# A one-column product for the sum of squares in a hybrid state-space and attention layer

## The chip, the cores and the metric

The kernel runs on one core of a Trainium2 chip. The metric is the device time of one execution in microseconds (us). Engines are named as in the profile: PE is the tensor engine, PEld its weight loads, DVE the vector engine, ACT the scalar engine, POOL GpSimd, SP the engine that issues most DMA transfers.

## The reference

One decoder layer over 2048 tokens and 16 meta tokens, 1024 features, float32. One input projection feeds two branches: a state-space scan with 16 heads in 4 groups, and gated linear attention with 4 heads. Each branch is normalised, projected, weighted with a gate and added; a last projection, the residual and a norm follow. The part around the change is the end of the state-space branch:

```python
y = jnp.concatenate([y_m, y_r], axis=1) + d_skip[:, None] * xs
y = y.reshape(b, l, D_SSD) * jax.nn.silu(z)
y_ssd = rmsnorm(y.reshape(b, l, SSD_GROUPS, D_SSD // SSD_GROUPS),
                ssd_norm_w.reshape(SSD_GROUPS, -1)).reshape(b, l, D_SSD)
```

So for each token and group the squares of 256 features are summed, and the features are scaled with the reciprocal root of their mean.

## The kernel before

The tokens are worked on in four blocks of 512. In a first half, each block goes through four state-space groups (`ssd_proj`, with `ssd_scan` for what follows a group's projections) and four attention heads (`gla_proj`, `gla_scan`). A second half, from about 1586 us on, does gates, branch projections and the output. Float32 products of the projections are made of three passes with operands split into a high and a low part (`accum`, lines 187 to 191).

The order of the first half is written with Python generators. `ssd_proj` and `gla_proj` yield after each piece, which is one projection tile of 24 passes on 512 columns in most cases. After each piece `step()` advances every scan that is under way to its next `yield`. So a `yield` in `ssd_scan` puts what follows one piece of PE's work later. PE and SP execute in the order written; for the other engines a planner that simulates the time line arranges the instructions, and each then executes in the order it was given.

A state-space group has six pieces: four projection tiles with a convolution (the last starts the scan), and two gate tiles `zs`. Its scan fetches decay rows from DRAM (`cb`, `yf`), makes the products of `bf` and `cf` for four chunks (L551), then works on the chunks one at a time (`before`, `after`: L565 to L599), and ends with the norm: features times gates (L615), squares (L616), their sum over the two tiles (L617), the sum over 128 partitions by eight passes on PE (L621, four products of float32 in two passes each, a column of ones as the moving operand), the reciprocal root (`rstd_of`, L232 on DVE and L233 on POOL), a store to DRAM and a load back that spreads the row over all partitions (L623, L625), and the last scaling (L630). Beside the scans run the gates of the attention (`gates`), the load of the next block (`load_u`) and sums for the second half (`make_sums`, whose POOL subtractions are L81).

Tiles come from pools with a fixed number of buffers: `tok4` 6, `sq` 5, `gg` 4, and three PSUM banks for each of `pj` and `pt`, two for `pc`.

Of the kernel before, what the change touches and what calls it, by code (L numbers as in the profile page):

```python
# [7 lines left out]
F32 = mybir.dt.float32  # L8
F32R = mybir.dt.float32r
# [5 lines left out]
P = 128  # L15
# [10 lines left out]
NSQ = 5  # L26
NT4 = 6
NACT = 4
NC1 = 6
LEVELS = (1, 2, 4, 8, 16, 32, 64)  # L30
NMSK = len(LEVELS)
# [10 lines left out]
def trunk_kernel(ctx: ExitStack, tc: tile.TileContext, xm, xmt, w_feat, w_tok, w_vm, w_br, w_o,  # L42
# [7 lines left out]
    def mk(pool, shape, dt, tag, **kw):  # L50
        cnt[0] += 1
        return pool.tile(shape, dt, tag=tag, name=f"{tag}_{cnt[0]}", **kw)
# [75 lines left out]
    def bank(pool, tag):  # L128
        return mk(pool, [P, 512], F32, tag)
# [100 lines left out]
    def rstd_of(ssq, n, scale):  # L230
        r = mk(sm, [P, 4], F32, "rstd")
        nc.vector.tensor_scalar(r[:, :n], ssq, scale, EPS, op0=ALU.mult, op1=ALU.add)  # L232
        nc.gpsimd.tensor_tensor(r[:, :n], r[:, :n], mhalf[:, :n], op=ALU.pow)  # L233
        return r
# [119 lines left out]
    def new_block(b, u):  # L354
        o = Block()
        o.b, o.u = b, u
        o.m0 = META if b == 0 else 0
        o.tt = o.m0 + BLK
        o.segs_all = [(0, o.tt // 2), (o.tt // 2, o.tt // 2)] if b == 0 else [(0, BLK)]
        o.segs_real = [(o.m0, BLK)]  # L360
        o.starts = [o.m0 + c * P for c in range(NCH)]
        o.chunks = ([(0, META)] if o.m0 else []) + [(a, P) for a in o.starts]
        o.ci0 = 1 if o.m0 else 0
        o.nck = len(o.chunks)
        for nm in ("tkd", "tkc", "wde", "dec"):
            setattr(o, nm, mk(bpool, [P, 5, NH], F32, nm, bufs=2))
        o.cumd = mk(dpool, [NH, BLK], F32, "cumd")
        o.ecud = mk(dpool, [NH, BLK], F32, "ecud")
        o.rstd = [mk(dpool, [P, NCH], F32, f"rstd{g}") for g in range(SG)]
        o.g_all = mk(bpool, [P, GH, META + BLK], F32, "g_all")  # L370
        o.gla = {}
        o.alr = mk(bpool, [P, 5, 48], F32, "alr")
        o.mov = lambda kt, a, n: tuple(t[:, kt, a:a + n] for t in u)
        return o


    def dt_chain(o, psd):
        m0, nck, ci0 = o.m0, o.nck, o.ci0
        tkd, tkc, wde, dec = o.tkd, o.tkc, o.wde, o.dec

        def t80(tag):
            return mk(sm, [P, 5, NH], F32, tag, bufs=1)[:, :nck]

        x = t80("dx")
        for i in range(nck):
            nc.vector.tensor_tensor(x[:, i], psd[i][:, 256:272], hv[:, 0], op=ALU.add)
            nc.scalar.activation(
                o.alr[:, i].rearrange("p (r c) -> p r c", c=16),
                psd[i][:, 272:288].unsqueeze(1).to_broadcast([P, 3, 16]), AF.Copy)
        e = t80("de")  # L390
        nc.scalar.activation(e, x, AF.Abs)
        nc.scalar.activation(e, e, AF.Exp, scale=-1.0)
        w1 = t80("dw")
        nc.vector.tensor_scalar(w1, e, 1.0, None, op0=ALU.add)
        ln = t80("dl")
        nc.scalar.activation(ln, w1, AF.Ln)
        nc.vector.scalar_tensor_tensor(e, w1, 1.0, e, op0=ALU.subtract, op1=ALU.subtract)
        nc.vector.tensor_tensor(ln, ln, e, op=ALU.subtract)
        dt = tkd[:, :nck]
        nc.vector.scalar_tensor_tensor(dt, x, 0.0, ln, op0=ALU.max, op1=ALU.add)  # L400
        nc.vector.tensor_tensor(x, dt, nega.unsqueeze(1).to_broadcast([P, nck, NH]), op=ALU.mult)
        yield
        ps = bank(pt, "pt")
        nc.tensor.matmul(ps[:, :nck * NH], tri, x.rearrange("p c h -> p (c h)"), start=True, stop=True)
        nc.vector.tensor_copy(tkc[:, :nck].rearrange("p c h -> p (c h)"), ps[:, :nck * NH])
        ps = bank(pt, "pt")
        if m0:
            nc.tensor.matmul(ps[:, :NH], ones[:META], x[:META, 0], start=True, stop=True)
        nc.tensor.matmul(ps[:, ci0 * NH:nck * NH], ones, x[:, ci0:].rearrange("p c h -> p (c h)"),
                         start=True, stop=True)  # L410
        psv = ps[:, :nck * NH].rearrange("p (c h) -> p c h", h=NH)
        nc.scalar.activation(dec[:, :nck], psv, AF.Exp)
        nc.vector.tensor_tensor(wde[:, :nck], psv, tkc[:, :nck], op=ALU.subtract)
        nc.vector.tensor_scalar(wde[:, :nck], wde[:, :nck], 0.0, None, op0=ALU.min)
        nc.scalar.activation(wde[:, :nck], wde[:, :nck], AF.Exp)
        nc.vector.tensor_tensor(wde[:, :nck], wde[:, :nck], dt, op=ALU.mult)
        yield
        ps = bank(pt, "pt")
        for c in range(NCH):
            nc.tensor.transpose(ps[:NH, c * P:(c + 1) * P], tkc[:, ci0 + c], ident)  # L420
        cr = mk(wk, [P, 3 + META + BLK], F32, "cin")[:NH, :BLK]
        nc.scalar.activation(cr, ps[:NH], AF.Copy)
        nc.scalar.dma_start(o.cumd, cr)
        er = mk(wk, [P, 3 + META + BLK], F32, "cin")[:NH, :BLK]
        nc.scalar.activation(er, ps[:NH], AF.Exp)
        nc.scalar.dma_start(o.ecud, er)
# [48 lines left out]
    def ssd_proj(o, g):  # L475
        m0, tt = o.m0, o.tt
        feats, zs = [], []
        if g == 0:
            yield from first_values(o)
        for j in range(4):  # L480
            ti = g * 4 + j
            pss = proj_feat(f"s{ti}", w_feat[T_SSD + ti], o.segs_all, o.mov)
            cin = mk(wk, [P, 3 + META + BLK], F32, "cin")
            acc = mk(wk, [P, META + BLK], F32, "acc")[:, :tt]
            nc.scalar.activation(cin[:, 0:3], tails[:, ti, :], AF.Copy)
            for ps, (a, n) in zip(pss, o.segs_all):
                nc.scalar.activation(cin[:, 3 + a:3 + a + n], ps[:, :n], AF.Copy)
                nc.scalar.activation(acc[:, a:a + n], ps[:, :n], AF.Identity, scale=hcw[:, ti, 3:4],  # L488
                                     bias=hcb[:, ti:ti + 1])
            nc.gpsimd.tensor_copy(tails[:, ti, :], cin[:, tt:tt + 3])  # L490
            for k in range(3):
                nc.vector.scalar_tensor_tensor(acc, cin[:, k:k + tt], hcw[:, ti, k:k + 1], acc,  # L492
                                               op0=ALU.mult, op1=ALU.add)
            if j % 2 == 0:
                two = pair_tile()
            f = two[:, j % 2]
            nc.scalar.activation(f[:, :tt], acc, AF.Tanh)
            nc.vector.scalar_tensor_tensor(f[:, :tt], f[:, :tt], 1.0, acc, op0=ALU.add, op1=ALU.mult)
            feats.append(f)
            if j == 3:  # L500
                begin(ssd_scan(o, g, feats, zs))
            yield
        for j in range(2):
            ti = 2 * g + j
            ps, = proj_feat(f"z{ti}", w_feat[T_Z + ti], o.segs_real, o.mov)
            zt = mk(wk, [P, BLK], F32, "gg", bufs=4)
            nc.scalar.activation(zt, ps, AF.Tanh, scale=0.5)
            nc.vector.scalar_tensor_tensor(zt, zt, 1.0, ps, op0=ALU.add, op1=ALU.mult)
            zs.append(zt)
            yield  # L510
# [7 lines left out]
    def ssd_scan(o, g, feats, zs):  # L518
# [4 lines left out]
        yf = mk(wk, [P, NCH, 256], F32, "tok4", bufs=NT4).rearrange("p c f -> p (c f)").rearrange("p (j t) -> p j t", j=2)  # L523
        for i in range(2):
            nc.scalar.dma_start(yf[64 * i:64 * i + 64], o.ecud[4 * g + i:4 * g + i + 3:2, :].unsqueeze(0).to_broadcast([64, 2, BLK]))
        yield
        hs = slice(4 * g, 4 * g + 4)

# [87 lines left out]
            nc.scalar.activation(zs[j], yf[:, j], AF.Square)  # L616
        nc.vector.tensor_tensor(zs[0], zs[0], zs[1], op=ALU.add)  # L617
        yield
        ps = bank(pt, "pt")
        for c in range(NCH):  # L620
            nc.tensor.matmul(ps[:, c:c + 1], zs[0][:, c::NCH], ones[:, :1], start=True, stop=True)  # L621
        r = rstd_of(ps[:, :NCH], NCH, 1.0 / 1024)
        nc.scalar.dma_start(o.rstd[g], r)  # L623
        rb = mk(wk, [P, BLK], F32, "gg", bufs=4)
        nc.scalar.dma_start(rb, o.rstd[g].rearrange("p c -> (p c)").unsqueeze(0).to_broadcast([P, BLK]))  # L625
        yield
        yield
# [37 lines left out]
    def gla_out_gates(o, h):  # L665
        t0 = T_GLA + 4 * h
        for j in range(2):
            ps, = proj_feat(f"g{t0 + 2 + j}", w_feat[t0 + 2 + j], o.segs_real, o.mov)
            gg = mk(wk, [P, BLK], F32, "gg", bufs=4)
            nc.scalar.activation(gg, ps, AF.Tanh, scale=0.5)  # L670
            nc.vector.scalar_tensor_tensor(gg, gg, 1.0, ps, op0=ALU.add, op1=ALU.mult)
            o.gla[h][1].append(gg)
            yield
# [566 lines left out]
```

## Time and profile before

| | us |
|---|---|
| median of 3 runs | 2375.83 (2368.9 to 2376.44) |
| the profiled execution | 2377.53 |
| its span, first to last instruction | 2375.7 |

| engine | busy us | share of the span |
|---|---|---|
| PE | 2270.2 | 96% |
| DVE | 1445.9 | 61% |
| ACT | 1091.8 | 46% |
| POOL | 679.7 | 29% |

The mean granted clock of TensorE is 0.979 of full speed. Passes on PE overlap, so that the sum of their durations is more than the busy time, and a busy PE can still be one at half clock; what a pass costs is read from the starts of one and the next. In rows of groups the numbers behind the bar are busy us, the mean ns of one instruction, and the engine's idle time before them with what ended it. In rows of waits they are us in total, times, and the longest.

### The profile page before, as it was taken

To read this page: it belongs to the slowest core of one execution; us is meant where nothing else is said; L and a number is where in the kernel's file an instruction comes from. 1 tells how busy PE (TensorE), PEld (TensorE's weight loads), DVE (VectorE), ACT (ScalarE), POOL (GpSimd) and SP (SyncE) were. 2 spreads that over 40 slices of the span, in tenths; PEclk is the share of its full clock that TensorE was granted. 3 is DMA by queue.
4 is the path that set the end of the run, shared out by engine and by line. 5 is a ranking of instruction groups with operands and counts; after the bars stand their busy time and mean duration, and the time that the engine had idled before them with its cause. 6 is when DMAs were issued, how large, how long until landed. Compare 5 with 4: busy or idle time off the path is not lost.

```text
span 2375.7 us, 34516 instructions
## 1 busy us (share of the span) xinstructions
PE 2270.2 (96%) x12009; PEld 1925.5 (81%) x12009; DVE 1445.9 (61%) x2467; ACT 1091.8 (46%) x2390; POOL 679.7 (29%) x681
## 2 busy tenths in 40 slices
PE   7999999999999999999999999979999999999998
PEld 6888888877888887888887789867888888888776
DVE  5676664466654456555356554455578854778776
ACT  4655554454433354433345333354545454554443
POOL 4343432212211112221112200027433355424231
PEclk9999999999999999999999999989999999999999
DMA  8776875777776677786587754457667876687743
GB/s 294 250 233 226 268 244 187 224 220 238 243 257 184 206 238 226 222 269 214 179 246 214 226 165 155 142 166 246 208 243 262 285 243 213 237 278 262 249 147 125
DMA packets 310877, 530.66 MB, mean 223 GB/s; under 512 B 30832, under 2 KB 146800, under 8 KB 310704
## 3 DMA queue, kind: packets, MB, share of 16 engines
q1 hardware_dynamic: 200400, 402.84, 52.6%
q10 hardware_dynamic: 110304, 125.63, 16.5%
q8 instruction: 94, 1.54, 0.3%
q14 instruction: 79, 0.65, 0.1%
HBM read 381.00 MB, written 147.36 MB: 222 GB/s over the span
## 4 chain that ended last, share of the span: by engine, by line
PE 71%; DMA 11%; DVE 6%; issue 4%; ACT 4%; POOL 2%; SPq 1%; ACTq 1%; POOLq 0%; DVEq 0%
PE pj L189 16%; PE pj L191 16%; PE pj L190 16%; PE pt L189 3%; PE pt L191 3%; PE pt L190 3%; PE pt L734 2%; DVE acc L492 2%; PE pc L190 2%; PE pc L189 2%; PE pc L191 2%; POOL wr L81 2%; DMA gg<-rstd 2%; DMA wr<-y 1%; PE pc L590 1%
## 5 line engine op out<-in xcount | busy, mean ns | idle before, releaser
L189 PE MATMUL pj<-u,whl 128*128 128x512 f32 (+1 forms) x1440 | 554.5, 385 | 6.1 <-ACT acc L488 3.9
L191 PE MATMUL pj<-u,whl 128*128 128x512 f32 (+1 forms) x1440 | 533.4, 370 | 0.8 <-POOL whl L170 0.8
L190 PE MATMUL pj<-u,whl 128*128 128x512 f32 (+1 forms) x1440 | 533.1, 370 | 0.0
L189 PEld LDWEIGHTS pj<-u,whl 128*128 128x128 f32 x1440 | 275.9, 192 | 52.5 <-ACT acc L488 5.6
L191 PEld LDWEIGHTS pj<-u,whl 128*128 128x128 f32 x1440 | 274.3, 190 | 47.7 <-POOL whl L170 1.1
L190 PEld LDWEIGHTS pj<-u,whl 128*128 128x128 f32 x1440 | 275.7, 191 | 42.4
L189 PE MATMUL pj<-b,a 128*128 128x512 f32 x640 | 254.5, 398 | 10.1 <-ACT sn L952 8.0
L190 PE MATMUL pj<-b,a 128*128 128x512 f32 x640 | 252.1, 394 | 1.8 <-DVE b L911 1.8
L191 PE MATMUL pj<-b,a 128*128 128x512 f32 x640 | 252.6, 395 | 0.0
L170 POOL TENSOR_TENSOR whl<-wr,whl 128x512 fp32r<-128x512 f32 (+1 forms) x100 | 133.4, 1339 | 191.1 <-ACT whl L169 168.5
L911 DVE TENSOR_TENSOR b<-br,b 128x512 fp32r<-128x512 f32 x196 | 152.7, 799 | 47.7 <-ACT b L910 45.2
L492 DVE SCALAR_TENSOR_TENSOR acc<-cin,hcw,acc 128x512 f32<-128x512 f32 (+1 forms) x192 | 159.9, 833 | 34.3 <-ACT acc L488 33.1
L926 POOL TENSOR_TENSOR as<-ar,ar 128x512 f32<-128x512 f32 x40 | 60.5, 1512 | 409.1 <-DMA ar<-in_w_br 151.0
L910 ACT ACTIVATE b<-br 128x512 fp32r<-128x512 f32 x196 | 119.2, 626 | 103.6 <-DMA br<-br_t 32.3
L936 DVE TENSOR_TENSOR a<-ar,a 128x512 fp32r<-128x512 f32 x160 | 126.8, 800 | 65.6 <-ACT a L935 63.5
L81 POOL TENSOR_TENSOR wr<-wr 128x256 f32<-128x256 f32 x80 | 69.0, 862 | 338.1 <-DMA wr<-y 142.6
L189 PEld LDWEIGHTS pj<-b,a 128*128 128x128 f32 x640 | 121.5, 190 | 38.5 <-ACT sn L952 10.2
L189 PE MATMUL pj<-whl,u 128*128 128x256 f32 (+1 forms) x480 | 143.7, 299 | 2.9 <-ACT u L307 1.5
L190 PEld LDWEIGHTS pj<-b,a 128*128 128x128 f32 x640 | 121.6, 190 | 29.0 <-DVE b L911 2.2
L191 PEld LDWEIGHTS pj<-b,a 128*128 128x128 f32 x640 | 121.5, 190 | 27.7
L191 PE MATMUL pj<-whl,u 128*128 128x256 f32 (+1 forms) x480 | 140.0, 292 | 1.4 <-DVE u L309 1.4
L190 PE MATMUL pj<-whl,u 128*128 128x256 f32 (+1 forms) x480 | 139.7, 291 | 0.0
(270 smaller groups left out, 4738.2 us busy)
## 6 DMA issues: line engine op xcount, KB each, us to landing
whl<-k_s SPq DMA_DIRECT2D x96, 512.0 KB, 4.5
whl<-k_g SPq DMA_DIRECT2D x96, 512.0 KB, 4.3
whl<-k_z SPq DMA_DIRECT2D x48, 512.0 KB, 3.7
wr<-in_w_feat SPq DMA_DIRECT2D x80, 256.0 KB, 4.2
whl<-k_v SPq DMA_DIRECT2D x36, 512.0 KB, 3.8
k_s<-whl SPq DMA_DIRECT2D x32, 512.0 KB, 3.5
cb<-cumd ACTq DMA_DIRECT2D x64, 256.0 KB, 5.4
k_g<-whl SPq DMA_DIRECT2D x32, 512.0 KB, 3.8
```

Source lines behind the costliest of these rows:

```text
L81: nc.gpsimd.tensor_tensor(o, x, y, op=ALU.subtract)
L170: nc.gpsimd.tensor_tensor(hl[:, 1], raw, hl[:, 0].bitcast(F32), op=ALU.subtract)
L189: nc.tensor.matmul(ps, sh, mh, start=first, stop=False, **kw)
L190: nc.tensor.matmul(ps, sh, ml, start=False, stop=False, **kw)
L191: nc.tensor.matmul(ps, sl, mh, start=False, stop=last, **kw)
L492: nc.vector.scalar_tensor_tensor(acc, cin[:, k:k + tt], hcw[:, ti, k:k + 1], acc, op0=ALU.mult, op1=ALU.add)
L590: nc.tensor.matmul(py[:, (2 + j) * P:(3 + j) * P], s_ssd[:, g, j * P:(j + 1) * P], cf[:, a:a + P], start=True, stop=True)
L734: nc.tensor.matmul(ps[:, r * P:(r + 1) * P], packed[0][:, r * P:(r + 1) * P], odd_even(half, m0 + (r + 2) * P, P // (2 * half), k_to_q - 2 ...
L910: nc.scalar.activation(t[:, 0], raw, AF.Copy)
L911: nc.vector.tensor_tensor(t[:, 1], raw, t[:, 0].bitcast(F32), op=ALU.subtract)
L926: nc.gpsimd.tensor_tensor(s1, a21, a22, op=ALU.add)
L936: nc.vector.tensor_tensor(t[:, 1], src, t[:, 0].bitcast(F32), op=ALU.subtract)
```

## The change

The sum of squares over the partitions becomes a product with one column of ones as the stationary operand, which gives a row of 512 sums. Its operand is split into a high part (ACT) and a low part (POOL) in a step of its own, and the product takes two passes. The row is copied from PSUM, stored to DRAM and loaded back as a column for each partition; `rstd_of` runs a step later on that. A `yield` more stands ahead of the scan's first products. The gate buffers become five, the decay tiles of a block have one buffer each, and three temporaries of the step-size chain use these tiles.

```diff
+NGG = 5
...
         for nm in ("tkd", "tkc", "wde", "dec"):
-            setattr(o, nm, mk(bpool, [P, 5, NH], F32, nm, bufs=2))
+            setattr(o, nm, mk(bpool, [P, 5, NH], F32, nm))
...
+        o.ssq = [mk(dpool, [P, NCH], F32, f"ssq{g}") for g in range(SG)]
...
-        e = t80("de")
+        e = wde[:, :nck]
...
-        w1 = t80("dw")
+        w1 = tkc[:, :nck]
...
-        ln = t80("dl")
+        ln = dec[:, :nck]
...
-            zt = mk(wk, [P, BLK], F32, "gg", bufs=4)
+            zt = mk(wk, [P, BLK], F32, "gg", bufs=NGG)
...
             nc.scalar.dma_start(yf[64 * i:64 * i + 64], o.ecud[4 * g + i:4 * g + i + 3:2, :].unsqueeze(0).to_broadcast([64, 2, BLK]))
+        yield
         yield
...
         nc.vector.tensor_tensor(zs[0], zs[0], zs[1], op=ALU.add)
         yield
+        sqh, sql = [mk(wk, [P, BLK], F32R, "sq", bufs=NSQ) for _ in range(2)]
+        nc.scalar.activation(sqh, zs[0], AF.Copy)
+        nc.gpsimd.tensor_tensor(sql, zs[0], sqh.bitcast(F32), op=ALU.subtract)
+        yield
         ps = bank(pt, "pt")
-        for c in range(NCH):
-            nc.tensor.matmul(ps[:, c:c + 1], zs[0][:, c::NCH], ones[:, :1], start=True, stop=True)
-        r = rstd_of(ps[:, :NCH], NCH, 1.0 / 1024)
+        for i, t in enumerate((sqh, sql)):
+            nc.tensor.matmul(ps[:1], ones_r[:, :1], t, start=i == 0, stop=i == 1)
+        rb = mk(wk, [P, BLK], F32, "gg", bufs=NGG)
+        nc.scalar.activation(rb[:1], ps[:1], AF.Copy)
+        nc.scalar.dma_start(o.ssq[g].rearrange("p c -> (p c)").unsqueeze(0), rb[:1])
+        s4 = mk(sm, [P, NCH], F32, "ssq")
+        nc.scalar.dma_start(s4, o.ssq[g])
+        yield
+        r = rstd_of(s4, NCH, 1.0 / 1024)
         nc.scalar.dma_start(o.rstd[g], r)
-        rb = mk(wk, [P, BLK], F32, "gg", bufs=4)
         nc.scalar.dma_start(rb, o.rstd[g].rearrange("p c -> (p c)").unsqueeze(0).to_broadcast([P, BLK]))
         yield
         yield
...
-            gg = mk(wk, [P, BLK], F32, "gg", bufs=4)
+            gg = mk(wk, [P, BLK], F32, "gg", bufs=NGG)
```

## The prediction

> **What bounds the kernel now.** I read the page first, then the chain, then the groups of TensorE's instructions, then the timeline around the line that the change removes, and last the clock in stretches.
>
> ```profile
> span 2375.7 us, 34516 instructions
> PE 2270.2 (96%) x12009; PEld 1925.5 (81%) x12009; DVE 1445.9 (61%) x2467; ACT 1091.8 (46%) x2390; POOL 679.7 (29%) x681
> PE 71%; DMA 11%; DVE 6%; issue 4%; ACT 4%; POOL 2%; SPq 1%; ACTq 1%; POOLq 0%; DVEq 0%
> 430.00:650.00 220.00, 213.19 (x1115) 176.01 (x1114) 132.42 (x258) 105.57 (x248) 52.27 (x76) 0.98 0.77 236
> ```
>
> The last row is the state-space stage of block 1 by itself (length, busy time of PE, its weight loads, DVE, ACT, POOL, then clock, DMA share, GB/s). PE is busy for 213 of 220 us while DVE has 132 and ACT 106. So in the stage that the change touches TensorE sets the pace, the others have room, and a microsecond taken from PE's stream there is worth about a microsecond, unless a wait of another engine reaches PE. These are the rows of PE that the change touches (busy, mean ns, then idle time before them and what ended it):
>
> ```profile
> L621 PE MATMUL pt<-ones_r,gg 128*128 128x1 f32 x128 | 30.3, 358 | 10.7 <-DVE gg L617 10.7
> L551 PE MATMUL pc<-act 128*128 128x128 f32 x128 | 22.3, 329 | 11.0 <-DVE act L498 11.0
> L779 PE MATMUL pt<-sq,ones_r 128*128 128x512 f32 x32 | 11.8, 453 | 0.0
> L587 PE MATMUL pc<-sq,c 128*64 128x128 f32 x512 | 42.1, 285 | 1.0 <-DVE sq L578 1.0
> ```
>
> The sum of squares is 128 passes with one moving column each, eight in each of 16 units (four groups in four blocks). It costs PE 30.3 us and another 10.7 us of waiting for the vector engine's sum.
>
> **Part one, the product itself.** A unit's eight passes become two passes of 512 columns against one column of ones, 32 in all. How dense such passes run is seen beside the old ones:
>
> ```profile
> 233.04 0.39 PE L189 MATMUL pj<-u,whl 128*128 128x512 f32 x1
> 233.27 0.40 PE L190 MATMUL pj<-u,whl 128*128 128x512 f32 x1
> 135.31 0.40 PE L191 MATMUL pj<-u,whl 128*128 128x512 f32 x1
> 135.54 1.80 PE L621 MATMUL pt<-ones_r,gg 128*128 128x1 f32 x8
> 137.27 0.69 PE L544 MATMUL pc<-c,bt 16*128 16x256 f32 x2
> ```
>
> A pass of 512 columns starts 0.23 us after the last; the old eight take from 135.54 to 137.27, 1.73 us. New passes at 0.23 would be 32 x 0.23 = 7.4 us; L779, which is the same form with 128 columns of ones in place of one, is 11.8 us for the same 32. No row has a single stationary column. If that were as slow again as L779 it would cost 23.6, which still is a gain. I take L779, its nearest row: 30.3 - 11.8 = 18.5 us saved, between 6.7 and 22.9.
>
> **Part two, the wait for the sum.** The three pieces put the high part (ScalarE) and the low part (GpSimd) one step of the order after the squares and the product another step later. The sum is late today in these units most of all:
>
> ```profile
> 521.48 2.03 PE L621 MATMUL pt<-ones_r,gg 128*128 128x1 f32 x8 [2.42 <-DVE gg L617]
> 901.16 2.03 PE L621 MATMUL pt<-ones_r,gg 128*128 128x1 f32 x8 [2.52 <-DVE gg L617]
> 1281.15 2.03 PE L621 MATMUL pt<-ones_r,gg 128*128 128x1 f32 x8 [3.49 <-DVE gg L617]
> L237 ACT ACTIVATE sq<-sq x16: 613/620/636, 284.1 to 1522.9; 128x512 fp32r<-128x512 f32 x16
> L170 POOL TENSOR_TENSOR whl<-wr,whl 128x512 fp32r<-128x512 f32 x92 | 126.6, 1380 | 179.4 <-ACT whl L169 156.7 <-PE pt L757 6.5 <-PE pt L191 6.1
> POOL wr L81 <- DMA wr<-y: 143.0, 19, 22.0
> ACT act L497 <- POOL wr L81: 23.1, 3, 7.7
> ```
>
> One more piece is 24 passes x 0.23 = 5.5 us of PE's time. Against it stand a copy of 0.62 and a subtraction of 1.38 us, so even the worst sum, 3.49 late, comes 5.5 - 3.49 - 2.0 = 0 us before it is needed: the 10.7 us go. The cover is thin. What is queued ahead on GpSimd is the preparation of later sums at L81, which waits for its loads, and its last row says that this has already held ScalarE for up to 7.7 us through GpSimd's queue. Price: nothing if GpSimd is free, 8 x 3 = 24 us if the low part is held by 3 us in half of the units. I take 2.
>
> **Part three, the first products a step later.** It moves L551, the transposes, the masks and everything that `before(0)` issues, the next load of `cb` on ScalarE's queue among it; the first loads stay where they are and gain 5.5 us of cover.
>
> ```profile
> PE pc L551 <- DVE act L498: 11.0, 7, 2.5
> ```
>
> PE's 11.0 us at L551 end with the vector op L498, which is at most 2.5 us late in its seven times: a whole piece covers it, and all 11.0 go. What is late next there is the vector op on these products, which nobody on PE needs for another piece.
>
> **Part four, the clock.** The stretches at half clock, in the view by stretches (length, PE busy, clock):
>
> ```profile
> 138.10:141.50 3.40, 3.40 (x17) 0.50 0.11 30
> 902.70:909.50 6.80, 6.80 (x23) 0.50 0.45 91
> 1332.80:1336.20 3.40, 3.40 (x14) 0.50 0.04 5
> sum 30.60, PE 30.11; mean PE 4.30
> 76.60:80.00 3.40, 3.40 (x12) 2.82 (x11) 2.32 (x5) 3.10 (x10) 0.30 (x1) 0.51 1.10 302
> 127.80:131.20 3.40, 3.40 (x13) 2.92 (x12) 2.70 (x6) 3.40 (x13) 0.25 (x1) 0.51 0.87 283
> ```
>
> The sum row is of seven stretches that begin during an L621 or within 1 us of its end; the last two follow a wait at L551. At half clock a stretch of dense work loses half: 30.6 / 2 = 15.3 and 6.8 / 2 = 3.4 us. I count 10 and 3, since other lulls may draw some; between 0 and 18.7. The first stretch follows passes without a wait (135.31 to 137.27 above has no idle time), so the one-column passes seem to count as little work.
>
> The Trainium skill's "TensorE: Matmul & The Clock Gate" (Part 1: The HAM clock gate) says that the clock halves after an idle window of about 3.4 us and comes back after a busy one. The stretch lengths agree; that 138.1 was drawn with no idle time does not. Read strictly, with busy instructions as busy, the rule would leave the halved stretches in place and make the sum 13 us less of a gain.
>
> **Part five, the longer way to the norm.** Instead of reading the sum from PSUM, ScalarE copies a row, stores it, loads it back as a column, and only then does the vector engine's L232 run; the store and the broadcast load of before follow. What these two DMAs cost is best told by the two that are there, the store (first row, issue to landing) and the broadcast load:
>
> ```profile
> DMA to landing us min/median/max: 1.4/2.8/5.6
> DMA to landing us min/median/max: 3.9/5.6/7.0
> DVE tok L630 <- DMA gg<-rstd: 58.5, 16, 6.1
> 673.16 1.42 DVE L630 SCALAR_TENSOR_TENSOR tok<-tok,hsw,gg 128x512 f32<-128x512 f32 x2 [4.86 <-DMA gg<-rstd]
> 676.61 0.71 PE L734 MATMUL pt<-act,c 128*128 128x128 f32 x4 [1.84 <-ACT c L728]
> 678.59 1.22 PE L734 MATMUL pt<-act,c 128*128 128x128 f32 x4 [1.27 <-ACT c L728]
> 677.40:684.20 6.80, 5.61 (x26) 5.61 (x27) 3.74 (x6) 2.30 (x5) 0.00 (x0) 0.50 0.65 251
> ```
>
> Store and load back take 2.8 + 5.6 = 8.4 us against one piece of 5.5, so the vector engine will wait some 3 us at L232, in order, with everything behind it: convolutions, evacuations, the decay products. ScalarE waits a little too, since the second DMA can't be issued before the first has landed. Two prices exist. In groups 0 to 2 the L630 waits of 3.7 us on average (58.5 / 16) reached PE only as the 1.0 us of L587: twelve new waits cost about 1 us. In group 3, whose end runs beside the linear-attention levels, the wait of 4.86 us at 673 cost PE 1.84 + 1.27 us and drew a half-clock stretch of 6.8 us, of which 3 us are lost: 6 us. Group 3 now has two waits there per block rather than one, and the norm's end has moved three steps on, to where the attention's splits are due. Four more such waits at between 0 and 6 us: I take 11 in all, between 0 and 24. Below nothing is excluded: no wait is removed from DVE but those for L621's result, which it never passed on.
>
> ScalarE gets two more operations of about 0.6 us and two issues in each unit, 16 x 1.9 = 30 us beside the 46% it has; GpSimd 16 x 1.38 = 22 us beside 29%. Hidden, by the stage's row above.
>
> ```profile
> L578 DVE TENSOR_TENSOR sq<-sq,sq x64: 678/692/1418, 79.1 to 1392.1; 128x512 f32<-128x512 f32 x64
> ```
>
> GpSimd's new subtraction has a second price: L578 takes 0.69 us, and up to 1.42 where it runs into a GpSimd operation. 16 x 0.7 = 11 us of vector time at most, for an engine with 88 us of room in a stage of 220; I count 2 us for it and ScalarE's waits together.
>
> The Trainium skill's "SBUF — State Buffer" (SBUF: two separate sides) has this as a rule: a vector operation with two SBUF inputs and a GpSimd operation take turns on one port pair, and the loser stands still. The maximum of 1.42 agrees. If every such stop reached PE, the sum would be 9 us less of a gain.
>
> **Part six, buffers.** The four decay tiles of a block lose their second buffer. Their last readers, group 3's scan, end in the first attention head, and the next block writes them three heads later: nothing, with three heads of PE work as cover. Temporaries of the step-size chain now live in them; that chain is serial anyway. The fifth gate buffer pays for gate tiles that live one step longer and for the row; without it the gates of the next group would wait. Nothing.
>
> **The sum.** Gains 18.5 + 10.7 + 11.0 + 10 + 3 = 53; costs 2 + 1 + 11 + 2 = 16; net 37 us. The profiled execution took 2377.5 us (span 2375.7 and 1.8 around it), 1.7 above the median of the runs: 2377.5 - 37 - 1.7 = 2339 us.
>
> **Rivals.**
> 1. The waits come back in part: the low part is late behind L81 (24 us in place of 2) and the rest as summed, net 15: 2361 us. For it stand L81's rows, against it that GpSimd is busy for 52 of 220 us. Chance 0.20.
> 2. Slower: the vector engine's in-order wait for the loaded-back column reaches PE not only beside the attention but in the state-space stage, at the price of 673, 6 us each. It decides from 53 / 6, that is 9 of the 16 units on; with all twelve of groups 0 to 2 it costs 72 and with group 3's 11 and 4 more us the sum is 53 - 87 = 34 us slower: 2410, and from 2385 on for fewer units. For it: 58.5 us of DVE waits of just this kind, and twice as many to come. Against it: the 1.0 us that reached L587. Chance 0.16.
> 3. The halved stretches stay, for they belong to lulls and not to L621: 13 less, 2352 us. Chance 0.06.
> 4. It does nothing: the weights' transfers (DMA share 0.77 in the stage) become the bound once PE asks faster: 2376 us. Against it, no DMA is among what ended the waits of the groups that use them, of which this is the first. Chance 0.06.
>
> ```profile
> L189 PE MATMUL pj<-u,whl 128*128 128x512 f32 (+1 forms) x1440 | 554.5, 385 | 6.1 <-ACT acc L488 3.9 <-ACT whl L169 2.1 <-ACT g_all L451 0.2
> ```
>
> **How the numbers follow.** The forecast has 0.52. A measurement of this kernel tells about 0.3%, 7 us, from no change. Faster: forecast, rivals 1 and 3, 0.78; same: rival 4, 0.06; slower: rival 2, 0.16. The low end takes the gains near their bounds (22.9 + 10.7 + 11.0 + 18.7 = 63, less 5): 2318. The high end takes in rivals 1, 3 and 4 and reaches rival 2's beginning, 2385. Some 0.06 lie below and 0.14 above.
>
> **What would show it.** Right: 32 passes of 512 columns in place of L621 with next to no idle time before them; L551 without its 11 us; a granted clock above 0.979; PE's idle time down most in the state-space stages; L232 waiting some 3 us on a DMA, 16 times, without a PE wait behind it except beside the attention. Wrong: PE waiting at the new product for GpSimd, or new waits at L565, L587 and L734 that end with vector operations just after L232; or a state-space stage of block 1 no shorter than 220 us.

## The result and the profile after

| | us | ratio to before, 95% interval |
|---|---|---|
| before, median of 6 runs | 2373.74 | |
| after, median of 6 runs (2385.19 to 2393.28) | 2389.77 | 1.0077 [1.005, 1.0104] |
| forecast | 2339, 2318 to 2385 | |

The change makes the kernel 0.8% slower. This is rival 2's side, at the start of its stretch. The profiled execution took 2389.14 us. A ratio is worked out from the single runs of both kernels and isn't the quotient of the two medians. All times here and below are of fast runs; slow ones (one of no_first_trip, 3159 us at a clock of 0.654, and one of the kernel before, 11242 us) are left out.

The page of the kernel after, span and busy time:

```profile
span 2386.7 us, 34422 instructions
PE 2248.6 (94%) x11913; PEld 1896.7 (79%) x11913; DVE 1452.0 (61%) x2467; ACT 1101.5 (46%) x2422; POOL 698.5 (29%) x697
```

PE is busy for 21.6 us less than before. But it stands idle for 2386.7 - 2248.6 = 138.1 us where it was 2375.7 - 2270.2 = 105.5. So 32.6 us of new waiting have eaten a gain of 21.6, and 11.0 more. The groups of PE's instructions say where the gain is and where most of the waiting is (busy, mean ns, then idle time before them by what ended it):

```profile
L628 PE MATMUL pt<-sq,ones_r 128*1 128x512 f32 x32 | 10.0, 395 | 0.0
L554 PE MATMUL pc<-act 128*128 128x128 f32 x128 | 17.0, 276 | 0.9 <-DVE s_ssd L599 0.9
L590 PE MATMUL pc<-sq,c 128*64 128x128 f32 x512 | 43.0, 290 | 27.2 <-DVE s_ssd L599 24.3 <-DVE tok L602 1.5 <-DVE rs L267 1.3
```

L628 is the new product: 10.0 us busy and no wait, where L621 had 30.3 and 10.7. L554 is the old L551, and its 11.0 us of waiting are 0.9. Below them stands the loss: L590, the old L587, waited 1.0 us before and 27.2 now, for the vector engine's update of the scan's state. Other waits of PE, and then those of DVE for the two loads back (total, times, longest):

```profile
PE pj L190 <- ACT g_all L453: 13.6, 4, 4.4
PE pt L808 <- DVE sq L796: 8.3, 3, 5.0
PE pj L450 <- ACT act L441: 6.4, 4, 2.5
```

```profile
DVE tok L642 <- DMA gg<-rstd: 53.4, 15, 5.8
DVE rstd L233 <- DMA ssq<-ssq: 33.1, 14, 4.3
```

The 13.6 and 6.4 us belong to the attention's gates and are taken up below; the 8.3 us at L808 stand in the attention beside the end of group 3. The second trip (L642, the old L630) makes the vector engine wait about as long as before, 53.4 after 58.5 us; the first trip adds 33.1. So the new waits of PE do not come from longer waits of DVE for the second load. What has changed is when these waits come, measured against what PE needs next. Pieces of the timeline show it (start, duration, instruction, and in brackets the idle time before), DVE first, then PE. The kernel before:

```profile
531.49 1.42 DVE L630 SCALAR_TENSOR_TENSOR tok<-tok,hsw,gg 128x512 f32<-128x512 f32 x2 [3.67 <-DMA gg<-rstd]
532.82 1.29 DVE L578 TENSOR_TENSOR sq<-sq,sq 128x512 f32<-128x512 f32 x2
...
535.79 0.41 DVE L596 TENSOR_TENSOR s_ssd<-s_ssd,pc 128x256 f32<-128x256 f32 x1
```

```profile
533.66 0.66 PE L587 MATMUL pc<-sq,c 128*64 128x128 f32 x8 [0.66 <-DVE sq L578]
```

And the kernel after:

```profile
568.63 0.74 DVE L494 SCALAR_TENSOR_TENSOR acc<-cin,hcw,acc 128x512 f32<-128x512 f32 x1
574.77 1.42 DVE L642 SCALAR_TENSOR_TENSOR tok<-tok,hsw,gg 128x512 f32<-128x512 f32 x2 [5.39 <-DMA gg<-rstd]
576.10 0.68 DVE L500 SCALAR_TENSOR_TENSOR act<-act,acc 128x512 f32<-128x512 f32 x1
576.70 0.42 DVE L571 TENSOR_TENSOR c<-pt,tkd 128x256 f32<-128x256 f32 x1
577.03 0.41 DVE L573 TENSOR_TENSOR c<-pt,wde 128x256 f32<-128x256 f32 x1
...
578.89 0.41 DVE L599 TENSOR_TENSOR s_ssd<-s_ssd,pc 128x256 f32<-128x256 f32 x1
```

```profile
574.63 0.39 PE L192 MATMUL pj<-u,whl 128*128 128x512 f32 x1
579.35 1.12 PE L590 MATMUL pc<-sq,c 128*64 128x128 f32 x8 [4.34 <-DVE s_ssd L599]
```

At 569.4 the vector engine reaches the last scaling of one group and waits 5.39 us for the broadcast load. Behind it in its order are the decay products (L571, L573) and the state update (L599) of the next group's scan, which starts 4.12 us after L642. PE can't go on with the next chunk before: it has issued the projection up to 574.63 and stands for 4.34 us. In the kernel before, work of the next group stood behind the load too, but that of its first chunk. There PE's next products needed the masked decays (L578), the first operation behind the scaling, and waited 0.66 us. Most of PE's waits at L590 are of the kind at 579.35: of thirteen in the timeline, ten, with 24.3 of the 27.2 us, end 3.4 to 5.6 us after the start of an L642 that had waited for its load. All ten stand in groups 0 to 2, of whose twelve waits for the load in the kernel before two reached PE's chunk products, with 0.66 and 0.37 us. The Trainium skill's "TensorE: Matmul & The Clock Gate" (Architectural detail: the array is 16× 32×32, not 1× 128×128) calls the vector engine's queue strictly first in, first out; the rows agree, since no other instruction of DVE stands between 569.4 and 574.77.

The granted clock of the profiled execution is next to unchanged, 0.979 before (all six runs of the kernel after have 0.977 to 0.980, those of the kernel before in the sessions below 0.976 to 0.984):

```profile
core 0: 2386.7 us, clock 0.980
```

And the state-space stage of block 1 (length, busy time of PE, its weight loads, DVE, ACT, POOL, clock, DMA share, GB/s), which took 220.00 us with PE busy for 213.19:

```profile
436.00:666.40 230.40, 213.04 (x1088) 173.87 (x1088) 124.16 (x248) 106.82 (x252) 51.61 (x76) 0.96 0.74 224
```

PE is busy as long as before, the stage is 10.4 us longer, and its clock is lower.

### The profile page after: what moved, and what is told of

It reads as the page before. It is cut to its first block, busy times and chain, and to the rows that moved or that the text cites. A ratio compares the mean times of both kernels' runs of the same rounds, so it can differ in the third digit from the quotient of the medians.

```text
span 2386.7 us, 34422 instructions
## 1 busy us (share of the span) xinstructions
PE 2248.6 (94%) x11913; PEld 1896.7 (79%) x11913; DVE 1452.0 (61%) x2467; ACT 1101.5 (46%) x2422; POOL 698.5 (29%) x697
## 5 line engine op out<-in xcount | busy, mean ns | idle before, releaser
L190 PE MATMUL pj<-u,whl 128*128 128x512 f32 (+1 forms) x1440 | 558.4, 388 | 25.0 <-ACT g_all L453 13.6
L190 PE MATMUL pj<-whl,u 128*128 128x256 f32 (+1 forms) x480 | 141.4, 295 | 3.7 <-DMA whl<-k_vm 1.9
L192 PE MATMUL pj<-whl,u 128*128 128x256 f32 (+1 forms) x480 | 138.0, 287 | 1.6 <-DVE u L310 1.6
L191 PE MATMUL pj<-whl,u 128*128 128x256 f32 (+1 forms) x480 | 137.7, 287 | 0.0
```

Source lines behind the costliest of these rows:

```text
L190: nc.tensor.matmul(ps, sh, mh, start=first, stop=False, **kw)
L191: nc.tensor.matmul(ps, sh, ml, start=False, stop=False, **kw)
L192: nc.tensor.matmul(ps, sl, mh, start=False, stop=last, **kw)
```

## The experiments

Line numbers differ by a few between kernels; the operation and the tiles name the same instruction. The kernels were measured in several sessions, each beside runs of the kernel before (medians 2370 to 2374 us). The last two columns are PE's idle time at the chunks' products and at the scan's first products in the profiled execution.

| kernel | median us | ratio to before, 95% interval | PE's wait at L590 (L587), us | at L554 (L551), us |
|---|---|---|---|---|
| before | 2373.74 | | 1.0 | 11.0 |
| later_start | 2369.23 | 0.9993 [0.9972, 1.0014] | 6.3 | 0.0 |
| product_only | 2416.23 | 1.0197 [1.016, 1.0234] | 37.7 | 29.4 |
| after | 2389.77 | 1.0077 [1.005, 1.0104] | 27.2 | 0.9 |
| no_trip | 2335.04 | 0.9844 [0.981, 0.9878] | 1.4 | 0.0 |
| no_first_trip | 2373.31 | 1.0007 [0.998, 1.0033] | 22.6 | 0.0 |
| no_second_trip | 2349.32 | 0.9913 [0.9884, 0.9941] | 4.8 | 0.0 |
| more_cover | 2398.76 | 1.0107 [1.0073, 1.014] | 28.7 | 0.7 |
| anchored | 2368.56 | 0.9985 [0.9966, 1.0004] | 0.4 | 0.0 |
| anchored_pool | 2370.28 | 0.9985 [0.9962, 1.0007] | 2.2 | 0.0 |
| on_chip | 2357.51 | 0.994 [0.992, 0.996] | 2.0 | 0.0 |
| on_chip_early | 2369.53 | 0.9987 [0.9968, 1.0006] | 1.5 | 34.7 |
| before_gates | 2373.64 | 1.0011 [0.9992, 1.003] | 20.8 | 0.0 |
| on_chip_gates | 2334.78 | 0.9833 [0.9806, 0.986] | 1.4 | 0.0 |

**The two halves of the change.** later_start is the kernel before with the one `yield` ahead of the first products; product_only is the kernel after without it.

```diff
 # later_start, from before; product_only takes this line out of after
             nc.scalar.dma_start(yf[64 * i:64 * i + 64], o.ecud[...]...)
+        yield
         yield
```

> The kernel before with one of the two edits alone: the scan's first products one piece later (one more yield ahead of them). Theory W (waits: the round trips through DRAM hold the vector and scalar engines in order, and the longer trip and its later landing cost what the product saves): the 11 us at L551 go, little else moves, 2355 to 2368 us. Rival O (order: the scan's later steps fall on other work, whatever the trip): this edit carries the loss, 2380 us or more.

> The changed kernel without the later start: product, split and the longer trip stay. W: the waits on both loads stay and land two steps later than in the kernel before, so most of the loss stays, 2375 to 2390 us. O: without the shifted start the product's saving shows, 2350 us or less.

The later start alone is worth nothing that can be measured. Its waits were exchanged: the 11.0 us at L551 are gone, and PE waits at the gates, where it had waited 0.2, and 5.3 us more at the chunks' products. Waits of PE in later_start:

```profile
PE pj L189 <- ACT g_all L451: 13.7, 4, 4.7
PE pj L448 <- ACT act L439: 4.5, 4, 2.0
```

The product alone costs 45 us (2416.23 - 2371.27), and with it the later start is worth 26 (2416.23 - 2389.77, between sessions). The waits of PE in product_only show what it takes away there:

```profile
PE pc L553 <- DVE act L500: 29.4, 13, 4.3
PE pc L589 <- DVE s_ssd L598: 19.5, 5, 6.0
PE pc L589 <- DVE tok L601: 17.5, 6, 4.8
```

So the product and its longer way carry the loss, and the later start hides part of it. product_only is slower than either expectation had it.

**Without the trip through DRAM.**

```diff
 # no_trip
-        nc.scalar.dma_start(o.ssq[g].rearrange("p c -> (p c)").unsqueeze(0), rb[:1])
-        s4 = mk(sm, [P, NCH], F32, "ssq")
-        nc.scalar.dma_start(s4, o.ssq[g])
         yield
-        r = rstd_of(s4, NCH, 1.0 / 1024)
-        nc.scalar.dma_start(o.rstd[g], r)
-        nc.scalar.dma_start(rb, o.rstd[g]...to_broadcast([P, BLK]))
...
-            nc.vector.scalar_tensor_tensor(yf[:, j], yf[:, j], hsw[:, i:i + 1], rb, ...)
+            nc.vector.scalar_tensor_tensor(yf[:, j], yf[:, j], hsw[:, i:i + 1], zs[1], ...)
 # no_first_trip: the sums on all partitions, the root straight from PSUM, one yield less
-            nc.tensor.matmul(ps[:1], ones_r[:, :1], t, start=i == 0, stop=i == 1)
+            nc.tensor.matmul(ps, ones_r, t, start=i == 0, stop=i == 1)
...
+        r = rstd_of(ps[:, :NCH], NCH, 1.0 / 1024)
 # no_second_trip: the first stays, the root is used as it is
+            nc.vector.scalar_tensor_tensor(yf[:, j], yf[:, j], r[:, j:j + 1], zs[1], ...)
```

> The changed kernel without the two stores to DRAM, the two loads and the reciprocal root; the last scaling reads a gate tile in the place of the norm, so the normalisation is left out. The product, the split, the copy of the row and the steps stay. W: what was forecast comes out, 2320 to 2345 us, with no wait of PE at L590. O: no better than the changed kernel by more than 10 us, 2378 to 2392 us.

> The changed kernel without the store and load of the sums: the product has all 128 columns of ones, and the root is taken of four columns of its result straight from PSUM, which leaves the norm's values out. The second store and load stay, as in the kernel before. W2: one wait of two goes in each unit, 2350 to 2372 us. A: as W2, for half of ScalarE's waits goes too. If the trips did not add up but the first alone cost: 2335 to 2345 us; if the second alone: 2380 us or more.

> The changed kernel with the first trip (store and load of the sums, root) and without the second: the last scaling takes two columns of the root and a gate tile, so the norm's values are left out. Without both trips 2335, without the first alone 2374. If each trip costs PE by itself: 2350 to 2358 us. If the two waits cost only together, one close behind the other: 2335 to 2345 us. If the first is the dear one: 2360 us or more.

Without both trips the kernel after takes 2335 us: 55 us hang on them. The first is worth 16 (2389.77 - 2373.31), the second 40 (2389.77 - 2349.32); the parts add up to about the whole. PE's wait at the chunks' products follows the second trip, not the first:

```profile
L590 PE MATMUL pc<-sq,c 128*64 128x128 f32 x512 | 42.1, 285 | 1.4 <-DVE sq L581 1.4
```

```profile
L590 PE MATMUL pc<-sq,c 128*64 128x128 f32 x512 | 42.9, 289 | 22.6 <-DVE tok L602 11.2 <-DVE s_ssd L599 11.2
```

```profile
L590 PE MATMUL pc<-sq,c 128*64 128x128 f32 x512 | 42.1, 285 | 4.8 <-DVE s_ssd L599 4.7
```

These are the groups of no_trip, no_first_trip and no_second_trip in this order. The second row is the telling one. no_first_trip has the two-pass product and only the way through DRAM that the kernel before has, and it is as slow as before: with the old trip two steps later, PE waits 22.6 us at the very instruction where it had waited 1.0. In its timeline nine waits at L590, with 22.4 of the 22.6 us, end 3.2 to 4.4 us after the start of a last scaling that had waited for its load.

**More cover, and why it isn't any.** A trip that is too long for its steps should be mended by a step more ahead of each waiting operation.

```diff
 # more_cover, from after
         nc.scalar.dma_start(s4, o.ssq[g])
         yield
+        yield
         r = rstd_of(s4, NCH, 1.0 / 1024)
...
         yield
         yield
+        yield
         for j in range(2):
```

> The changed kernel with one more yield between the load of the sums and the reciprocal root, and one more ahead of the last scaling: the same trip, 5.5 us more cover for each load. W: the vector engine's waits of 33 and 53 us all but vanish, PE's 27 us at L590 with them, 2345 to 2365 us. O: each further step moves more onto other work, 2388 us or more.

Nothing changed: 2398.76 us, and the same waits in the vector engine:

```profile
DVE tok L644 <- DMA gg<-rstd: 52.1, 15, 9.1
DVE rstd L233 <- DMA ssq<-ssq: 36.1, 13, 4.7
```

The instructions in the two traces say why. In more_cover each of PE, DVE, ACT and GpSimd has the list of the kernel after, operation for operation and tile for tile. A `yield` binds PE and SP alone, and neither has an instruction in these two steps. The planner that arranges the other engines places L233 and L642; as I read it, it puts them where its own simulation has the load landed, and on the chip the load lands later. (As the lists are equal, 1.0077 and 1.0107 also show how far two sessions can differ.)

**Anchored.** To bind the vector operations to their step, each takes an operand that PE makes in that step: a column of 1/1024, and the columns of `hsw`, each by a small product with the identity.

```diff
 # anchored, from more_cover
+        pa = bank(pt, "pt")
+        nc.tensor.matmul(pa[:, :1], ident, inv[:, :1], start=True, stop=True)
-        r = rstd_of(s4, NCH, 1.0 / 1024)
+        r = rstd_of(s4, NCH, pa[:, 0:1])
...
+        pa = bank(pt, "pt")
+        nc.tensor.matmul(pa[:, :2], ident, hsw[:, 2 * g:2 * g + 2], start=True, stop=True)
-            nc.vector.scalar_tensor_tensor(yf[:, j], yf[:, j], hsw[:, i:i + 1], rb, ...)
+            nc.vector.scalar_tensor_tensor(yf[:, j], yf[:, j], pa[:, j:j + 1], rb, ...)
 # anchored_pool: the four transfers are issued by gpsimd, not by scalar
```

> The kernel with more cover, and the two vector operations that wait for loads (root of the loaded-back column, last scaling) take their scalar from PSUM, from a product of one or two columns that PE makes in the piece meant for them: 32 products of two passes, some 0.45 us each, 14 us of PE. Theory W2 (placement: a yield binds PE and SP alone; the planner puts the vector operation where it believes the load has landed, which is earlier than it lands, so the wait moves with the code and more cover changed nothing): both waits fall under 10 us in all, PE's waits at L590 too, 2345 to 2370 us. Rival A (ScalarE is what holds PE: it stands at the second DMA's issue until the first has landed): the vector waits go but PE's stay, 2385 us or more.

> The anchored kernel with the two stores and two loads of the norm issued by GpSimd in place of ScalarE. Anchored stands some 33 us above the kernel without a trip, of which 9 are the anchors' products. Rival A (ScalarE standing at the issue of the second DMA of each trip, 31 us in its profile, reaches PE): 2345 to 2358 us. If that waiting is hidden, or GpSimd's queue pays for it: 2364 us or more.

Now the place does move, and 21 to 30 us come back (from 2389.77 of the kernel after and 2398.76 of more_cover to 2368.56), though the anchors cost PE 8.8 us. DVE's waits, then PE's groups, in anchored:

```profile
DVE tok L650 <- PE pt L647: 31.1, 10, 4.6
DVE rstd L235 <- PE pt L639: 16.6, 10, 3.5
```

```profile
L592 PE MATMUL pc<-sq,c 128*64 128x128 f32 x512 | 42.1, 285 | 0.4 <-DVE sq L583 0.4
L647 PE MATMUL pt<-hsw,cst 128*128 128x2 f32 x32 | 4.4, 208 | 0.0
L639 PE MATMUL pt<-inv,cst 128*128 128x1 f32 x32 | 4.4, 208 | 0.0
```

The vector operations wait for PE's anchor, by then not for a load, and PE waits 0.4 us at the chunks' products. The expectation that both waits fall under 10 us was wrong: together they are 47.7 us still, but at this place they don't hold PE there. With the transfers issued by GpSimd the time is the same, 2370.28: that ScalarE stands while it waits to issue them isn't what costs. Anchored is still 34 us above no_trip (2368.56 - 2335.04). The anchors' 8.8 explain a part, and two waits of the attention's products for L650 (3.5 and 3.1 us) another; what the other 18 or so are was not settled.

**The norm without DRAM.** With all 128 columns of ones the sums stand on every partition, and ScalarE makes the root there.

```diff
 # on_chip, from after; on_chip_early is the same without the later start
-            nc.tensor.matmul(ps[:1], ones_r[:, :1], t, start=i == 0, stop=i == 1)
+            nc.tensor.matmul(ps, ones_r, t, start=i == 0, stop=i == 1)
         rb = mk(wk, [P, BLK], F32, "gg", bufs=NGG)
+        nc.scalar.activation(rb, ps, AF.Ln, scale=1.0 / 1024, bias=epsc)
+        nc.scalar.activation(rb, rb, AF.Exp, scale=-0.5)
...
```

> The changed kernel with no DRAM on the way: all 128 columns of ones, so that every partition holds the sums, and the root as exp(-0.5 ln x) on ScalarE for 128x512, two operations and two table loads in each unit, some 3.8 us of ScalarE, 60 in all. Both theories: 2330 to 2350 us, if ScalarE's 60 us stay hidden; if the table loads reach PE, 2355 to 2375 us.

> The same without the later start of the scan's first products. If the later start is worth its 11 us at L551 here: 8 to 15 us more than with it. If, as in the kernel before, it only trades that wait for one at the attention's gates: within 5 us of it.

on_chip is 0.6% faster than before, and the later start is worth 12 us in it (2369.53 - 2357.51). Without it, in on_chip_early, the norm doesn't go through DRAM and the kernel is still no faster than before. PE then waits for the vector engine at the scan's first products, 34.7 us where the kernel before has 11.0:

```profile
L556 PE MATMUL pc<-act 128*128 128x128 f32 x128 | 23.1, 337 | 34.7 <-DVE act L503 34.7
```

So the trips are not the only thing that the new norm costs. What on_chip pays is seen on ScalarE, in table loads at its two new lines:

```profile
L633 ACT ACT_TABLE_LOAD x16 | 20.5, 1283 | 1.5 <-issue 1.3
L634 ACT ACT_TABLE_LOAD x11 | 14.1, 1283 | 0.2
```

The Trainium skill's "ScalarE: Activation LUTs" (Table sets: the hidden batching unit) says that one set holds both functions, so that a logarithm and an exponential after it need one load; here 11 of the 16 pairs took two at these lines, and in the other five an exponential of the scan (L583) stands between and took the second; the whole trace has 57 table loads, the kernel before 25. Whether they reach PE isn't shown. PE's waits in on_chip are now led by the gates:

```profile
PE pj L193 <- ACT g_all L456: 12.8, 4, 4.3
PE pj L453 <- ACT act L444: 7.2, 4, 2.3
```

But no_trip, without the new loads and 22 us faster, has as much there (12.7 and 9.4 us), so these waits are not what sets the two apart; that stays open.

**The gates a piece later.** If the later start only exchanged its waits for those of the gates, they should go by the same means.

```diff
 # on_chip_gates, from on_chip; before_gates, from later_start
     def gates(o):
         m0, tt, chunks, g_all = o.m0, o.tt, o.chunks, o.g_all
+        yield
```

> The kernel before with the later start and, new, the attention's gates begun one piece later as well (a yield at the head of gates). If the later start was worth nothing because its 11 us at L551 came back as waits of PE at the gates' products (18 us in its profile: L189 after L451 13.7, L448 4.5), those go now: 2350 to 2362 us. If the loss lies elsewhere: 2366 to 2375 us.

> The kernel with the norm on the chip, and the gates one piece later. If the gates' waits (20 us in its profile) are an exchange for those at L551: 2335 to 2348 us. If they come back elsewhere: 2352 us or more.

In before_gates it is worth nothing. PE's wait at the chunks' products, then DVE's for the broadcast load:

```profile
PE pc L589 <- DVE sq L580: 19.7, 3, 8.3
```

```profile
DVE tok L632 <- DMA gg<-rstd: 49.4, 15, 5.4
```

The gates' waits are nearly gone, and 19.7 us stand at the chunks' products once more. All three of these waits end 2.2 us after the start of a last scaling that had waited 5.30, 1.23 and 4.26 us for its broadcast load. I read them as the effect of that load in front, as above; but each is some 3 us longer than the load's wait, so that the load isn't all of it, and no run took it out of this kernel. With the norm on the chip the same line is worth 23 us (2357.51 - 2334.78, between sessions): on_chip_gates takes 2334.78, 0.9833 [0.9806, 0.986] of before, the lowest time here, below both before and after. Its stage of block 1:

```profile
426.50:636.70 210.20, 206.15 (x1087) 169.47 (x1087) 126.03 (x250) 114.64 (x259) 51.03 (x74) 0.99 0.80 242
```

9.8 us shorter than before, with PE busy for all but 4.05 us and the clock at 0.99.

## Why the prediction was wrong

**What bounds the kernel: right.** PE sets the pace in the state-space stage, and what was lost was lost as waits of PE there.

**Part one: right, and low.** 20.3 us saved for 18.5; a pass against a single stationary column takes 395 ns, and against 128 columns at the same line of no_first_trip 396. **Part two: right.** All 10.7 us went, and the low part on GpSimd was never late; rival 1 falls.

**Part three: the row was right, the gain was not.** The 11.0 us at L551 went, and "what is late next there" was answered wrongly: later_start shows 13.7 + 4.5 us at the gates. I looked for the next late operation on the moved products only, and not among the scans that run beside them. The gates a piece later then pass it on to the chunks' products in the kernel before. This alone doesn't sink the forecast: no_trip has the gates' waits too and comes to 2335 us, 4 below the forecast, which had 11 for the trip in it.

**Part four: wrong for this kernel.** I counted 13 us, and the clock went from 0.979 to 0.980. The change took some lulls of PE away and made others. Four new stretches at half clock begin within 1.6 us of the end of a wait at L590 that one of the ten loads caused (length, PE busy, clock, DMA share, GB/s):

```profile
579.20:582.60 3.40, 3.25 (x15) 0.50 0.65 252
627.00:630.40 3.40, 3.40 (x10) 0.50 0.00 0
961.50:964.90 3.40, 3.40 (x16) 0.50 0.33 128
1009.30:1012.70 3.40, 3.40 (x11) 0.50 0.00 0
```

In the kernels without these waits the clock does rise, to 0.984 in no_trip and 0.987 in on_chip_gates. Rival 3, that the stretches stay, is near what the clock shows here: the old ones at L621 went and others came. The reading that one-column passes count as little work is not borne out. Two of the seven stretches counted for L621 begin later than 1 us after its end (1.8 us for the one at 189.3, 1.4 us for the one at 1332.8), and in later_start, which keeps the one-column passes without a wait before them, no stretch begins during one or within 1 us of its end.

**Part five: the step that failed.** I priced the longer way through DRAM at 11 us, 10 of them in group 3 and 1 in the twelve units of groups 0 to 2, and put the later place of the trip that was already there at nothing for these twelve. For group 3 the size was near: 8.3 us at L808, which end 2.8 to 6.1 us after the start of an L642 there. For groups 0 to 2 it was not: 24.3 us at L590 behind ten of the twelve. By the runs without them, both trips cost 55 us, the added one 16 and the old one, in its new place, 40. Two things in this part were wrong.

First, the 1.0 us of L587 was read as the price of a vector wait for a load. It was the price of such a wait at that place in the vector engine's order, where PE's next products needed what stood first behind the load. The change put the norm's end some steps further into the next group's scan, where PE needs the state update or the sum beside it (L599, L602), and in those ten places the update starts 3.0 to 5.2 us after the last scaling. The 55.2 us of vector waits of no_first_trip then cost 22.6 us at L590, where 58.5 had cost 1.0. I had noted that the end moves "three steps on" and used it for group 3 alone; the ten waits above stand in groups 0 to 2, where the next group's scan runs beside the norm. How much of the second trip's 40 us the kernel before already paid stays open, since no run took it out there.

Second, I set 8.4 us of transfers "against one piece of 5.5" as if the `yield` gave the vector engine that piece. For DVE, ScalarE and GpSimd it gives nothing: more_cover, with a piece more for each trip, is the same program. The wait at L233 was forecast at some 3 us, 16 times, and is 2.4 us, 14 times (33.1 / 14), and from the issue of the store to L233 it is 6.9 us (median of the 14) where 8.4 was forecast, so that the size came out near by luck while the reason for it was mistaken.

**Part six:** none of PE's longest waits names a decay tile; no run tested the buffers by themselves.

**Rival 2 is what happened.** Its mechanism, the vector engine's in-order wait reaching PE in the state-space stage, was named with its place, and its lines to watch named L587, the old L590. It named the first trip as the cause, where the second does more, and at 6 us for each unit its price was too high: ten waits of 0.9 to 4.3 us reached L590. The evidence set against it, the 1.0 us, was the number that the change itself invalidated. A chance of 0.16 was too little for a mechanism with twice the waits to come and an argument against it that hung on one row.

## What to carry to other kernels

The cost of an in-order wait isn't in the wait but in what is queued behind it: before moving a step that ends in a load, list the instructions that will stand behind it on its engine and ask who on the bounding engine needs them. Find out which engines a hand-written order binds; where a planner places the rest by its own idea of when a transfer lands, a step of "cover" in the source may cover nothing, unless an operand ties the instruction to that step. And a wait that is taken away is a gain only when the stage gets shorter: the later start alone moved 11 us from one row to others and gained nothing, while with the norm on the chip it was worth 12 us and, with the gates later too, 35 (2369.53 - 2334.78).

## What the hardware showed that was not expected

A weight load of one column is cheaper than one of 128, but far from 128 times, and the pass behind it takes the same time. L628 in the kernel after, and then in no_first_trip (minimum, median, maximum ns):

```profile
L628 PEld LDWEIGHTS pt<-sq,ones_r x32: 81/83/86, 152.0 to 1448.8; 128*1 128x1 f32 x32
L628 PE MATMUL pt<-sq,ones_r x32: 390/396/398, 152.2 to 1449.1; 128*1 128x512 f32 x32
```

```profile
L628 PEld LDWEIGHTS pt<-sq,ones_r x32: 187/188/192, 149.8 to 1434.4; 128*128 128x128 f32 x32
L628 PE MATMUL pt<-sq,ones_r x32: 390/397/403, 149.9 to 1434.6; 128*128 128x512 f32 x32
```

It takes 83 ns for one column and 188 for 128. And the two loads back differ little in time, though one brings 2 KB and the other, the broadcast to all partitions, 256 KB. One load of the sums in the kernel after, its issue and the operation that waited for it:

```profile
560.15 0.34 ACTq L633 DMA_DIRECT2D ssq<-ssq  x1
565.16 0.17 DVE L233 TENSOR_SCALAR rstd<-ssq 128x4 f32<-128x4 f32 x1 [4.34 <-DMA ssq<-ssq]
```

From the issue to the start of the operation that waited it is 3.9 us for the sums (median of 14, 1.6 to 5.8) and 5.1 us for the broadcast (median of 15, 3.9 to 6.6). I had priced the first by the second, at 5.6.
